# A gated delta rule scan in a two-layer encoder: its chunk attention matrices as 128x128 tiles

## The chip, the cores and the metric

The kernel runs as one program on one core of a Trainium2 chip. The metric is device microseconds (us) from start to end of one execution; the number of a kernel is the median of its runs. The chip's engines work side by side and each takes its own instructions in the order of the program: PE multiplies matrices (PEld is its loading of weights, which can run beside a product), DVE, ACT and POOL are the three engines for elementwise work, and SP issues most transfers. An engine that waits for another holds up everything behind it in its own order.

## The reference

Layer 0 is chunked softmax attention, layer 1 a gated DeltaNet; each is followed by a dense squared-ReLU MLP, with norms and residuals. The change is in layer 1. With 1024 frames in 16 chunks of 64, and 8 heads of width 128, its last step scans over the chunks:

```python
qk = jnp.einsum('bhnid,bhnjd->bhnij', q, k) * decay      # 64 x 64 for each head and chunk
...
def step(state, inp):
    u_c, w_c, qk_c, qd_c, kd_c, gl_c = inp
    v_new = u_c - jnp.einsum('bhck,bhkv->bhcv', w_c, state)
    o_c = jnp.einsum('bhck,bhkv->bhcv', qd_c, state) + jnp.einsum('bhij,bhjv->bhiv', qk_c, v_new)
    state = state * gl_c[..., None, None] + jnp.einsum('bhck,bhcv->bhkv', kd_c, v_new)
    return state, o_c
```

## The kernel before

Everything is float32. The dense products of layer 1 (the q, k, v and z panels, then two panels of the output matrix; tiles `acc`) take their operands as pairs of a high part and a remainder (`xhi`, `xlo`, `whi`, `wlo`): three products 128x512 in place of one. Between these dense products the code weaves small tasks, written as generators: `dn_prep_keys`, `dn_prep_queries` and `dn_prep_values` make a head's matrices, `dn_inverses` and `dn_solves` the triangular inverse (the solves are long runs of DVE work), `dn_scans` the scan, `dn_outs` the head's output. A planner (`turn`, `Clock`) decides after each dense product which task may go one step further, by its own estimate of each engine's time and by priorities; the order that it finds is fixed in the program. Two scans run interleaved, one over the even heads and one over the odd.

A chunk pair `p` has 128 frames: chunk `e = 0` lies on partitions 0 to 63 and `e = 1` on 64 to 127. One step of the scan (`dn_scans`) for a head and a chunk is:

- PE, "WQ product": `ps` (128x128, name `s1`, shown as `s<-st,WQ`) from the state `st`. One half of its rows is w times the state, the other half is q times the state. It opens an accumulation that is not yet closed.
- DVE, `vn<-vb,s`: the new values, from the w half of `ps`. `vn` has 128 rows, of which the other chunk's 64 are zero for good.
- PE, "kd product" (`s<-vn,kd`): into `s2`, for the next state.
- PE, "qk product" (`s<-vn,qk`): added to the other half of `ps`. Its weights are `qk[:, p]`, 128 partitions and 64 columns, the one chunk's block over the other's. The product therefore gives 64 rows, and `tile_position=(0, 64 - 64 * e)` says which half of the array's columns, and of `ps`'s rows, they take.
- DVE, `st<-st,gl,s`: the next state. ACT, `o<-s`: the finished half of `ps` to the output tile.

A float32 product 128x128 runs in two passes, so the profile counts two loads and two products for each. There are 8 heads and 16 chunks, so 128 qk products, 120 kd and 120 WQ products (the first chunk has no state, the last makes none). `dn_prep_queries` fills `qk` for a head: DVE multiplies the diagonal blocks of q times k by the decay, four operations for a head. `dn_gates` makes the tiles that live through the layer, and POOL fills them with zeros.

Of the kernel before, what the change touches and what calls it, by code (L numbers as in the profile page):

```python
# [7 lines left out]
F32 = mybir.dt.float32  # L8
# [3 lines left out]
ALU = mybir.AluOpType  # L12
# [4 lines left out]
P = 128  # L17
# [21 lines left out]
def wide(col, p, n):  # L39

    return col.rearrange("p (q o) -> p q o", o=1).broadcast_to([p, col.shape[-1], n])
# [164 lines left out]
class Trunk:  # L206
# [1499 lines left out]
    def dn_gates(self):  # L1706
        nc, a, rhs = self.nc, self.a, self.drhs
        d1, db = self.d1, self.db
# [18 lines left out]
        for v in self.vn:  # L1727
            for e in range(2):
                nc.gpsimd.memset(v[e][64 - 64 * e : 128 - 64 * e], 0.0)
        yield  # L1730
        abd = self.abd

# [3 lines left out]
        def t64(name):  # L1736
            used.append(name)
            return room[(len(used) - 1) // 8][:NQ, (len(used) - 1) % 8]
# [13 lines left out]
        x, y, z, z2, pz, be = t64("gx"), t64("gy"), t64("gz"), t64("gz2"), t64("gp"), t64("be")  # L1752
# [53 lines left out]
        ps = tp[:, :256].rearrange("p (n h q) -> p n h q", n=4, h=8)  # L1806
# [369 lines left out]
    def dn_prep_queries(self):  # L2176
        nc, db = self.nc, self.db
        for h in range(8):
            yield from self.until("q", h)
            qT = self.heads.pop(("q", h))  # L2180
            dc = self.dq.tile([P, HB], F32, name=self.nm("dc"), tag="dc").rearrange("p (q t) -> p q t", t=64)
            nc.sync.dma_start(dc, self.decay[h])
            if h == 0:
                yield from self.until("u", 6)
            row = self.whole("row")
            self.bcast(row, self.grow[2, h])

            v = self.d1.tile([P, 8], F32, name=self.nm("lv"), tag="lvq", bufs=2)
            yield from self.l2_sums(qT, 128.0 ** -0.5, v)
            yield from self.rsqrt_few(v, 8, "q")  # L2190
            self.heads["rq", h] = self.got
            yield from self.until("rk", h // 4)
            nc.gpsimd.tensor_tensor(dc, dc, wide(self.rk[:, h], P, 64), ALU.mult)
            yield
            yield from self.until("kn", h)
            kn = self.heads["kn", h]
            if h >= 2:
                yield from self.until("scan", h - 2)
            qk = db.tile([P, 8, 64], F32, name=self.nm("qk"), tag="qk")
            for q in range(2):  # L2200
                s = slice(4 * q, 4 * q + 4)
                tp = yield from self.take("tp")
                ps = tp.rearrange("p (q t) -> p q t", t=P)
                for t in range(4):
                    c = slice((4 * q + t) * P, (4 * q + t + 1) * P)
                    nc.tensor.matmul(ps[:, t], kn[:, c], qT[:, c], start=True, stop=True)
                yield
                for e in range(2):
                    r = slice(64 * e, 64 * e + 64)
                    nc.vector.tensor_tensor(qk[r, s], ps[r, :, r], dc[r, s], ALU.mult)  # L2210
                self.give("tp", tp)
                yield
            WQ = db.tile([P, 8, 4, 64], F32, name=self.nm("WQ"), tag="WQ")
            nc.gpsimd.tensor_tensor(
                WQ[:, :, 1:3], qT.rearrange("p (q e t) -> p q e t", e=2, t=64),
                row.rearrange("p (q e t) -> p q e t", e=2, t=64), ALU.mult)
            self.heads["qq", h] = WQ, qk
            self.mark("queries", h)
            self.mark("q", "used", h)
            yield  # L2220
# [44 lines left out]
    def dn_scans(self, odd):  # L2265

        nc, db = self.nc, self.db
        for h in range(odd, 8, 2):
            yield from self.until("values", h)
            u, WQ, qk, kd = self.heads.pop(h)  # L2270
            if h:
                yield from self.until(*(("solve", 1) if h == 1 else ("out", h - 2)))
            o = self.heads["o", h] = db.tile([P, 8, P], F32, name=self.nm("o"), tag="o")
            st = None
            for c in range(16):
                p, e = c // 2, c % 2
                r, x = slice(64 * e, 64 * e + 64), slice(64 - 64 * e, 128 - 64 * e)
                wq = WQ[:, p].rearrange("p f t -> p (f t)")[:, P * e : P * e + P]
                ps = yield from self.take("s1")
                vn = self.vn[odd][e]  # L2280
                if st is None:
                    nc.vector.tensor_copy(vn[r], u[r, p])
                else:
                    nc.tensor.matmul(ps, wq, st, start=True, stop=False, skip_group_check=True)
                    yield
                    nc.vector.tensor_tensor(vn[r], u[r, p], ps[r], ALU.subtract)
                yield
                if c < 15:
                    s2 = yield from self.take("s2")
                    nc.tensor.matmul(s2, kd[:, p], vn, start=True, stop=True)  # L2290
                ready = self.clock.end
                nc.tensor.matmul(ps[x], qk[:, p], vn, start=st is None, stop=True,
                                 tile_position=(0, 64 - 64 * e), skip_group_check=True)
                self.clock.end = ready
                yield
                if c < 15:
                    nst = db.tile([P, P], F32, name=self.nm("st"), tag=f"st{odd}")
                    if st is None:
                        nc.vector.tensor_copy(nst, s2)
                    else:  # L2300
                        nc.vector.scalar_tensor_tensor(nst, st, self.gl[:, h, c : c + 1], s2, ALU.mult, ALU.add)
                    self.give("s2", s2)
                    st = nst
                ready = self.clock.end
                nc.scalar.activation(o[r, p], ps[x], AF.Copy)
                self.give("s1", ps)
                self.clock.end = ready
                if c == 7:
                    self.done["half", h] = self.clock.now + 2.0
                yield  # L2310
            self.mark("scan", h)
            yield
# [180 lines left out]
```

## Time and profile before

| | us |
| --- | --- |
| median of 3 runs (2691.9 to 2694.18) | 2693.39 |
| the profiled execution | 2695.22 |
| its span, first to last instruction | 2693.4 |
| PE busy in the span | 2559.9 (95%) |
| PEld, DVE, ACT, POOL busy | 2068.5, 1884.9, 1224.6, 1302.7 |
| mean granted clock of PE | 0.982 of full speed |

The profiled execution lies 1.8 us above the median, and its span 1.8 us below its own time. Busy PE is modelled: products overlap, so a product's length in the profile says less than the distance from its start to the start of the next. The scan's steps lie between 1467 and 1913 us of the span; what follows is the output product and the second MLP.

### The profile page before, as it was taken

How to read it: one execution, taken by the hardware profiler on the slowest of the kernel's cores; microseconds unless marked ns; L12 is line 12 of the kernel's file. 1: busy time of each engine (PE TensorE's matmuls, PEld its weight loads, DVE VectorE, ACT ScalarE, POOL GpSimd, SP SyncE). 2: the span in 40 equal slices, each digit the busy share in tenths (PEclk: the TensorE clock that was granted, in tenths of full speed). 3: DMA queues.
4: the chain of work that ended last, by engine and by line, in shares of the span. 5: the costliest groups of instructions: out<-in, count | busy, mean ns of one | idle time of the engine just before them, and what ended most of it. 6: DMA issues, size and time to landing. Idle time of an engine off the chain costs nothing.

```text
span 2693.4 us, 36113 instructions
## 1 busy us (share of the span) xinstructions
PE 2559.9 (95%) x12638; PEld 2068.5 (77%) x12638; DVE 1884.9 (70%) x3287; ACT 1224.6 (45%) x2269; POOL 1302.7 (48%) x1096
## 2 busy tenths in 40 slices
PE   8999999989999999998888999999999999999997
PEld 6888888868888777776767778787677888777775
DVE  6666566575545999987398856665575544799997
ACT  6665667343434534444653333333334444444443
POOL 2443446143223788885554323222132223588886
PEclk9999999989999999999989999999999999999998
DMA  4222235223333432322642212112323332433322
GB/s 156 65 75 66 66 90 170 97 97 125 114 106 102 156 110 94 106 90 84 171 117 75 69 55 75 56 61 102 102 91 136 103 117 98 157 106 101 97 99 78
DMA packets 141814, 271.78 MB, mean 101 GB/s; under 512 B 49264, under 2 KB 55856, under 8 KB 141632
## 3 DMA queue, kind: packets, MB, share of 16 engines
q1 hardware_dynamic: 120752, 227.51, 27.0%
q10 hardware_dynamic: 20880, 41.97, 4.1%
q8 instruction: 99, 1.62, 0.3%
q14 instruction: 83, 0.68, 0.1%
HBM read 193.24 MB, written 67.80 MB: 97 GB/s over the span
## 4 chain that ended last, share of the span: by engine, by line
PE 75%; DVE 15%; issue 5%; ACT 2%; POOL 1%; DMA 1%; SPq 0%; DVEq 0%; ACTq 0%; POOLq 0%
PE y L1000 22%; PE acc L161 18%; PE z L1000 10%; PE acc L1000 6%; PE s L161 3%; PE tp L161 3%; PE po L161 2%; PE pt L161 2%; PE sp L161 2%; DVE x L1365 2%; DVE a L1006 2%; PE acc L272 2%; PE acc L273 2%; PE acc L271 2%; DVE ft L161 1%
## 5 line engine op out<-in xcount | busy, mean ns | idle before, releaser
L161 PE MATMUL acc<-xhi,whi 128*128 128x512 f32 (+1 forms) x904 | 375.1, 415 | 7.0 <-DVE xp L161 7.0
L161 PE MATMUL acc<-xlo,whi 128*128 128x512 f32 (+1 forms) x904 | 374.9, 415 | 0.7 <-DVE xlo L387 0.7
L161 PE MATMUL acc<-xhi,wlo 128*128 128x512 f32 x896 | 370.2, 413 | 2.0 <-POOL wlo L161 2.0
L1015 POOL TENSOR_TENSOR s<-wraw 128x256 f32<-128x256 f32 (+1 forms) x93 | 101.2, 1088 | 557.6 <-DMA wraw<-in_w_up_dram 398.9
L161 POOL TENSOR_TENSOR wlo<-wraw,whi 128x512 fp32r<-128x512 f32 x126 | 167.2, 1327 | 266.8 <-ACT whi L161 199.9
L1009 ACT ACTIVATE xhi<-r 128x512 fp32r<-128x512 f32 x224 | 135.8, 628 | 264.4 <-POOL r L1012 212.6
L1006 DVE TENSOR_TENSOR wlo<-wraw,whi 128x512 fp32r<-128x512 f32 (+1 forms) x184 | 201.7, 1096 | 51.6 <-ACT whi L1009 48.2
L1000 PE MATMUL y<-xhi,whi 128*128 128x512 f32 x504 | 202.8, 402 | 12.4 <-DVE ssum L1083 8.7
L1000 PE MATMUL y<-xhi,wlo 128*128 128x512 f32 x504 | 202.1, 401 | 13.0 <-DVE wlo L1006 13.0
L1012 POOL TENSOR_TENSOR r<-r,r 128x512 f32<-128x512 f32 x124 | 204.0, 1647 | 12.9 <-DVE xlo L1006 12.6
L1000 PE MATMUL y<-xhi,a 128*128 128x512 f32 x488 | 179.7, 409 | 25.6 <-DVE x L1365 25.1
L161 PEld LDWEIGHTS acc<-xhi,whi 128*128 128x128 f32 (+1 forms) x904 | 172.6, 191 | 38.6 <-issue 6.5
L1000 PE MATMUL y<-xlo,whi 128*128 128x512 f32 x504 | 201.6, 400 | 0.0
L161 PEld LDWEIGHTS acc<-xhi,wlo 128*128 128x128 f32 x896 | 172.3, 192 | 32.4 <-issue 5.1
L161 PEld LDWEIGHTS acc<-xlo,whi 128*128 128x128 f32 (+1 forms) x904 | 172.9, 191 | 30.2 <-issue 5.0
L1365 DVE TENSOR_TENSOR x<-y,x 128x512 f32<-128x512 f32 x240 | 163.8, 682 | 9.4 <-PE y L1000 7.8
L1009 ACT ACTIVATE whi<-wraw 128x512 fp32r<-128x512 f32 (+2 forms) x191 | 143.6, 766 | 34.8 <-ACT g L1086 11.8
L1083 DVE TENSOR_TENSOR ssum<-acc,nt 128x512 f32<-128x512 f32 x32 | 22.1, 692 | 190.4 <-PE acc L1000 190.4
L161 POOL TENSOR_SCALAR pr<-pr,rs 128x640 f32<-128x640 f32 (+4 forms) x128 | 88.3, 693 | 129.6 <-DVE rs L161 98.3
L1000 PEld LDWEIGHTS y<-xhi,a 128*128 128x128 f32 x488 | 91.5, 188 | 72.0 <-DVE x L1365 51.2
L161 POOL TENSOR_TENSOR cy<-cy,cz 128x512 f32<-128x512 f32 x48 | 69.0, 1437 | 159.6 <-DVE cz L161 133.0
L161 ACT ACTIVATE o<-s 64x128 f32<-64x128 f32 x128 | 34.7, 271 | 212.7 <-PE s L161 137.2
(348 smaller groups left out, 7186.0 us busy)
## 6 DMA issues: line engine op xcount, KB each, us to landing
wraw<-in_w_up_dram SPq DMA_DIRECT2D x64, 512.0 KB, 3.4
wraw<-in_w_down_dram SPq DMA_DIRECT2D x64, 512.0 KB, 3.9
r<-gd SPq DMA_DIRECT2D x112, 256.0 KB, 2.7
gd<-ssum ACTq DMA_DIRECT2D x64, 256.0 KB, 2.0
gd<-g ACTq DMA_DIRECT2D x64, 256.0 KB, 2.3
wraw<-in_w_in_dram SPq DMA_DIRECT2D x32, 512.0 KB, 3.5
wraw<-in_w_qkv_dram SPq DMA_DIRECT2D x30, 512.0 KB, 3.3
x<-xd SPq DMA_DIRECT2D x24, 512.0 KB, 4.8
```

The costliest lines, as they stand in the source:

```text
L161: return call(*args, **more)
L271: nc.tensor.matmul(ps, hi[:, k], xh, start=(k == 0), stop=False)
L272: nc.tensor.matmul(ps, hi[:, k], xl, start=False, stop=False)
L273: nc.tensor.matmul(ps, lo[:, k], xh, start=False, stop=(k == KT - 1))
L1000: nc.tensor.matmul(ps, w[:, k], x, start=bool(first and f), stop=bool(last and e), skip_group_check=True)
L1006: self.nc.vector.tensor_tensor(lo, src, hi.bitcast(F32), ALU.subtract)
L1009: self.nc.scalar.activation(hi, src, AF.Copy)
L1012: self.nc.gpsimd.tensor_tensor(out, x, y, ALU.subtract)
L1015: self.nc.gpsimd.tensor_tensor(out, x, y, ALU.add)
L1083: nc.vector.tensor_tensor(g, c, t, ALU.add)
L1365: nc.vector.tensor_tensor(x, ps, x, ALU.add)
```

## The change

The chunk attention matrices become 128x128. Two tiles `qk0` and `qk1` (P x 8 x 128) are made once in `dn_gates`, used by even and odd heads in turn, and replace the two-buffer tile `qk` (P x 8 x 64). Half of each is filled with zeros by POOL, two operations a tile. `dn_prep_queries` writes a chunk's 64x64 block beside the zeros: rows 0 to 63 in columns 64 to 127, rows 64 to 127 in columns 0 to 63. The qk product then has weights 128x128 and is added to the whole of `ps`: in the rows that it had before it adds what it added before, and in the other half, which DVE has read by then, it adds zeros.

```diff
+        self.qks = [d1.tile([P, 8, P], F32, name=f"qk{n}") for n in range(2)]
+        for qk in self.qks:
+            for e in range(2):
+                nc.gpsimd.memset(qk[64 * e : 64 * e + 64, :, 64 * e : 64 * e + 64], 0.0)
...
-            qk = db.tile([P, 8, 64], F32, name=self.nm("qk"), tag="qk")
+            qk = self.qks[h % 2]
...
-                    nc.vector.tensor_tensor(qk[r, s], ps[r, :, r], dc[r, s], ALU.mult)
+                    nc.vector.tensor_tensor(qk[r, s, 64 - 64 * e : P - 64 * e], ps[r, :, r], dc[r, s], ALU.mult)
...
-                nc.tensor.matmul(ps[x], qk[:, p], vn, start=st is None, stop=True,
-                                 tile_position=(0, 64 - 64 * e), skip_group_check=True)
+                nc.tensor.matmul(ps, qk[:, p], vn, start=st is None, stop=True, skip_group_check=True)
```

The order on PE in the middle of the scan, before (a row is an instruction, its output, its inputs and the output's partitions x columns; the numbers tell buffers apart):

```order
L161 MATMUL s_3362_15312<-vn_12203,kd_14835 128x128
L161 MATMUL s_3359_15299<-vn_12203,qk_14841 64x128
L161 MATMUL acc_15220<-xhi_11784,whi_14969 128x512
L161 MATMUL s_3364_15319<-st_15307,WQ_14261 128x128
L161 MATMUL acc_15220<-xlo_11785,whi_14969 128x512
L161 MATMUL acc_15220<-xhi_11784,wlo_14970 128x512
L161 MATMUL acc_15328<-xhi_11758,whi_14969 128x512
L161 MATMUL s_3367_15330<-st_15316,WQ_14956 128x128
L161 MATMUL s_3368_15332<-vn_12204,kd_14052 128x128
L161 MATMUL s_3364_15319<-vn_12204,qk_14058 64x128
```

and the same place now:

```order
L161 MATMUL s_3359_15315<-vn_12203,kd_14839 128x128
L161 MATMUL s_3356_15302<-vn_12203,qk_12210 128x128
L161 MATMUL acc_15223<-xhi_11784,whi_14972 128x512
L161 MATMUL s_3361_15322<-st_15310,WQ_14265 128x128
L161 MATMUL acc_15223<-xlo_11785,whi_14972 128x512
L161 MATMUL acc_15223<-xhi_11784,wlo_14973 128x512
L161 MATMUL acc_15331<-xhi_11758,whi_14972 128x512
L161 MATMUL s_3364_15333<-st_15319,WQ_14959 128x128
L161 MATMUL s_3365_15335<-vn_12204,kd_14057 128x128
L161 MATMUL s_3361_15322<-vn_12204,qk_12211 128x128
```

Nothing moved: each qk product stands where it stood and has 128 rows where it had 64. The same holds for every instruction of PE, DVE and ACT. The one difference in the order is on POOL, at the start of layer 1, where `dn_gates` fills its tiles (`vn` the values, `fz` the solve's matrix, `wlo` a remainder of weights). Before:

```order
L161 MEMSET vn_12204 64x128
L161 MEMSET vn_12205 64x128
L161 MEMSET fz_12275 128x1024
L161 MEMSET fz_12275 128x32
L161 TENSOR_TENSOR wlo_12280<-wraw_12126,whi_12279 128x512
```

and now:

```order
L161 MEMSET vn_12204 64x128
L161 MEMSET vn_12205 64x128
L161 MEMSET qk_12210 64x8x64 x2
L161 MEMSET qk_12211 64x8x64 x2
L161 MEMSET fz_12281 128x1024
L161 MEMSET fz_12281 128x32
L161 TENSOR_TENSOR wlo_12286<-wraw_12126,whi_12285 128x512
```

Four fills were put in, ahead of the solve's fills and of a remainder of weights.

## Rows read from the trace of the kernel before

**Rows 1.** Stretches: length, busy us of PE, PEld, DVE, ACT, POOL; clock; DMA.

```profile
1460.00:1500.00 40.00, 39.17 (x309) 32.36 (x305) 34.55 (x91) 14.67 (x30) 13.49 (x12) 1.00 0.20 57
1500.00:1540.00 40.00, 37.93 (x229) 27.99 (x228) 39.10 (x61) 11.36 (x22) 12.46 (x9) 1.00 0.11 34
1540.00:1890.00 350.00, 344.41 (x2129) 276.26 (x2128) 209.92 (x543) 122.90 (x271) 103.58 (x76) 1.00 0.22 72
1890.00:1913.00 23.00, 19.92 (x92) 13.72 (x91) 14.40 (x39) 8.19 (x20) 6.37 (x5) 0.93 0.41 126
```

**Rows 2.** PE timeline: start us, length us, instruction, passes; the place shown above.

```profile
1601.10 0.38 PE L161 MATMUL s<-vn,kd 128*128 128x128 f32 x2
1601.41 0.43 PE L161 MATMUL s<-vn,qk 128*64 128x128 f32 x2
1601.78 0.50 PE L161 MATMUL acc<-xhi,whi 128*128 128x512 f32 x1
1602.11 0.38 PE L161 MATMUL s<-st,WQ 128*128 128x128 f32 x2
1602.25 0.48 PE L161 MATMUL acc<-xlo,whi 128*128 128x512 f32 x1
1602.56 0.39 PE L161 MATMUL acc<-xhi,wlo 128*128 128x512 f32 x1
...
1603.03 0.38 PE L161 MATMUL s<-st,WQ 128*128 128x128 f32 x2
1603.24 0.39 PE L161 MATMUL s<-vn,kd 128*128 128x128 f32 x2
```

**Rows 3.** PE timeline, a qk product that another small product follows.

```profile
1869.93 0.43 PE L161 MATMUL s<-vn,qk 128*64 128x128 f32 x2
1870.29 0.49 PE L161 MATMUL s<-vn,kd 128*128 128x128 f32 x2
```

**Rows 4.** PEld timeline beside group 2: weight loads, idle time ahead in brackets.

```profile
1600.87 0.42 PEld L161 LDWEIGHTS s<-vn,kd 128*128 128x128 f32 x2
...
1601.41 0.19 PEld L161 LDWEIGHTS s<-vn,qk 128*64 128x64 f32 x2
1601.77 0.19 PEld L161 LDWEIGHTS acc<-xhi,whi 128*128 128x128 f32 x1 [0.17 <-issue]
```

**Rows 5.** Weight loads by tile: ns minimum/median/maximum, first and last start.

```profile
L161 PEld LDWEIGHTS s<-vn,qk x256: 132/136/232, 1467.8 to 1912.4; 128*64 128x64 f32 x128
L161 PEld LDWEIGHTS s<-vn,kd x240: 186/188/335, 1467.3 to 1909.2; 128*128 128x128 f32 x120
```

**Rows 6.** DVE timeline beside group 2: a state's update.

```profile
1601.52 0.35 DVE L161 SCALAR_TENSOR_TENSOR st<-st,gl,s 128x128 f32<-128x128 f32 x1 [1.04 <-PE s L161]
```

**Rows 7.** Waits of PE, 1540 to 1890 us: total us, times, longest.

```profile
PE s L161 <- DVE vn L161: 3.1, 3, 1.5
PE s L161 <- DVE rt L161: 2.5, 1, 2.5
```

**Rows 8.** POOL timeline where dn_gates fills its tiles.

```profile
1244.14 1.84 POOL L161 MEMSET Zh<- 128x1024 f32 x2
1246.04 0.92 POOL L161 MEMSET vn<- 64x128 f32 x4
...
1248.53 1.28 POOL L161 TENSOR_TENSOR wlo<-wraw,whi 128x512 fp32r<-128x512 f32 x1 [0.46 <-ACT whi L161]
```

**Rows 9.** PE timeline: the first product that reads this wlo.

```profile
1263.00 0.39 PE L161 MATMUL acc<-xhi,wlo 128*128 128x512 f32 x1
```

**Rows 10.** DVE groups by line: us busy, mean ns, idle ahead.

```profile
L161 DVE TENSOR_TENSOR qk<-tp,dc 64x256 f32<-64x256 f32 x32 | 13.4, 420 | 5.0 <-PE tp L161 4.7
L161 DVE TENSOR_TENSOR vb<-tp,gcols 128x512 f32<-128x512 f32 x16 | 11.0, 687 | 5.8 <-PE tp L161 5.6
```

**Rows 11.** PE timeline, the first qk product, which opens its own accumulation.

```profile
1467.81 0.43 PE L161 MATMUL s<-vn,qk 128*64 128x128 f32 x2
1468.17 0.50 PE L161 MATMUL acc<-xlo,whi 128*128 128x512 f32 x1
```

## The prediction

> **What bounds the kernel now.** The change touches the scan alone, so I read the stretch in which the scan runs, 1460 to 1913 us, first by busy time [rows 1]. From 1540 to 1890 us PE is busy 344.41 of 350 us, DVE 209.92, ACT 122.90 and POOL 103.58, at the full clock. PE is the bound there, and time taken from PE is time taken from the kernel, as long as the others keep up. From 1500 to 1540 us it is different: DVE is busy 39.10 of 40 us, because the second triangular solve runs, and PE with 37.93 is level with it. From 1460 to 1500 us PE is ahead (39.17 against 34.55). From 1890 us on PE is idle for 3.1 of 23 us: the dense work runs out and the last head's steps wait for each other.
>
> Second, the waits of PE from 1540 to 1890 us [rows 7]: four waits, 5.6 us in all, each for DVE. So 98% of the stretch is PE's own.
>
> Third, PE's timeline around a qk product, read by starts, since busy lengths overlap [rows 2]. A kd product starts at 1601.10, the qk product at 1601.41, the dense product behind it at 1601.78, and what follows that at 1602.11. These distances are 0.31, 0.37 and 0.33 us, 1.01 in all. Now the same with a full-width product of the same type: from the WQ product at 1603.03 to kd at 1603.24 are 0.21, from WQ at 1602.11 to the dense product at 1602.25 are 0.14, and from there to the next at 1602.56 are 0.31. So a half-width product starts later, runs longer and delays what comes behind it.
>
> Fourth, the loads of weights at the same place [rows 4]. The full-width load of kd begins at 1600.87, before its product at 1601.10: it runs beside the dense product ahead. The half-width load begins with its product, at 1601.41, when kd is done, and the dense load behind it sits idle 0.17 us for nothing the profile shows. On both sides of the half-width product nothing is loaded ahead. I read this as the array being emptied whenever the shape of its tiles changes.
>
> **The change part by part.**
>
> *The qk product takes the whole array.* It then has the shape, type and passes of kd and WQ, so I price it by their rows. Where a dense product follows, the three distances go from 1.01 to 0.21 + 0.14 + 0.31 = 0.66 us. I take 0.34 us saved, since other places of the timeline read 0.34 as often as 0.35. In the program's order this is so for 96 of the 128. In the other 32 a small product follows: a kd in 15, as here [rows 3], elsewhere a WQ, a product or transpose of the preparation, or in 2 another qk. From qk at 1869.93 to kd at 1870.29 are 0.36 us; with the 0.31 ahead of it 0.67, against twice 0.21 for full-width products; 0.25 saved. The sum for PE alone is 96 x 0.34 + 32 x 0.25 = 40.6 us, or 0.317 for a product.
>
> Where these products lie, counted by their passes in the four stretches of [rows 1]: 7, 6, 107 and 8. The 40.6 us so divide into 2.2, 1.9, 33.9 and 2.5.
>
> *What of it the end sees.* From 1500 to 1540 us DVE has 0.9 us to give; I take 0.5 of the 1.9. From 1460 to 1500 us I take 1.5 of the 2.2. From 1890 us on the chain WQ, `vn`, kd, `st` sets the pace and qk is beside it; I take 1.0 of the 2.5. In the long stretch a wait can grow where a qk product stood between DVE's work and its reader on PE, because the reader now comes sooner. In [rows 6] a state is ready at 1601.87 and its WQ product starts at 1602.11, 0.24 us later, with one qk product between. Under the change that product comes at 1601.10 + 0.66 = 1601.76, before the state is there: a new wait of about 0.1 us. Of the 101 WQ products of that stretch, counted in the timeline, five have 0.24 us to spare with a qk product between, two have 0.30, and the others with one between 0.66 or more; a kd product with under 0.4 us to spare has none between. That is 1 us of new waits. At the four waits of [rows 7] DVE is behind with its own work, and what PE gains in the run-up is lost there: some 0.4 us each, 1.5 together. So 33.9 - 2.5 = 31.4 us, and in all 1.5 + 0.5 + 31.4 + 1.0 = 34.4.
>
> *Loads of full width.* Each load grows from 136 to 188 ns [rows 5], 256 of them by 52 ns, 13.3 us of PEld. I cost this at nothing, as PEld is busy 276 of 350 us [rows 1] and kd's full-width loads run beside the dense products [rows 4]. Without that cover it is the whole 13.3.
>
> The Trainium skill speaks against the change here. Its page "TensorE: Matmul & The Clock Gate", section "LDWEIGHTS (loading the stationary operand)", says that a load's time goes by its columns alone; as an estimate from that page 64 more columns cost 53 ns at 1.2 GHz, and the rows agree with it. By that rule alone the sum would be a loss of 13 us.
>
> *Zeros.* POOL fills four times 64 partitions x 512 elements. The nearest rows are 0.23 us for `vn` (128 elements) and 0.92 for `Zh` (1024) [rows 8]; four of them cost 0.9 to 3.7 us, about 2. Behind them in POOL's queue stand the solve's fills and a remainder of weights, written by 1249.81; PE reads that at 1263.00 [rows 9]. With 13 us to spare it costs nothing; without them 2 us.
>
> *The copy into `qk`.* The same 256 elements now go to blocks 128 apart; the input was strided already. It takes 420 ns [rows 10]. Between no change and the 687 ns of an operation with twice the elements, 32 copies cost DVE 0 to 8.5 us. I take 0, the elements being the same, and the upper end would fall mostly in stretches where DVE is idle 40%.
>
> *The zeros added to the other half of `ps`* need a wait for DVE's reading, but the kd product just ahead on PE waits for the same `vn` already. The order on PE, DVE and ACT is unchanged, so no queue is passed.
>
> **The rivals.**
>
> *DVE takes over.* PE gets faster by a tenth where products are dense, and DVE with its in-order work stops PE more often. For: from 1500 to 1540 us it does, and all waits of [rows 7] are for DVE. Against: it is 60% busy in the long stretch. If half of the 33.9 is lost, the gain is 17 + 3 = 20 us: 2673.
>
> *The distances don't come from the tile's shape* but from adding to an accumulation that another product opened. For: qk does that each time, kd never. Then the change gains nothing: 2693. Against: the very first qk product opens its own accumulation, and the dense product behind it still starts 0.36 us later [rows 11].
>
> *The load becomes the path.* A full-width load that stands between two products of one `vn` does not fit beside a product of two short passes, and PE waits for it. At 52 ns a load, with nothing won, 2693 + 13 = 2707. It decides only if the load can't start before the product ahead has ended. Against: from WQ to kd are 0.21 us [rows 2], with two loads of 188 ns in them, so it starts before.
>
> The Trainium skill has one more on this side. Its page "TensorEngine Tiling (Array Packing)", section "Overview", gives up to twice the speed where the stationary free dimension is at most 64, as it is before. By that the half-width form should be the better one; in this case two halves never run at once, because a full-width product lies between nearly all of them.
>
> **How the numbers follow.** The forecast is 2693.4 - 34.4 = 2659 us; for a profiled execution like the one before 2695.2 - 34.4 = 2661. I give it 0.80, for gains from 27 to 42. DVE taking over, gains from 6 to 27, has 0.12; no effect 0.04; the load 0.04. The range goes from all of 40.6 and about 1 more, 2652, to the time of DVE taking half, 2673. A measurement of this kernel can tell about 0.2% from no change, 5.4 us. Faster 0.92, same 0.04, slower 0.04.
>
> **What would show it.** In the profile after, the distance from the start of a qk product to the dense product behind it should read 0.14 us, and kd to qk 0.21; qk's loads should read 188 ns and start before their product; PEld's idle behind qk should be gone. The scan should end some 34 us sooner, and everything behind it keep its length. Waits of PE for `vn` and `st` should total under 10 us in the long stretch. It is wrong if the distances stay, or if PE's waits for DVE grow by more than 10 us.

## The result and the profile after

The kernel after took 2659.49 us in the median of four runs (2656.81 to 2660.27), the kernel before 2692.74 on the same chip (2691.9 to 2694.18): a ratio of 0.987, 95% interval 0.9855 to 0.9884. The forecast was 2659. In the profiled execution the span fell from 2693.4 to 2657.9 us.

First PE's timeline of the kernel after, at the place of [rows 2]: start us, length us, instruction, passes.

```profile
1594.58 0.38 PE L161 MATMUL s<-vn,kd 128*128 128x128 f32 x2
1594.80 0.39 PE L161 MATMUL s<-vn,qk 128*128 128x128 f32 x2
1594.94 0.48 PE L161 MATMUL acc<-xhi,whi 128*128 128x512 f32 x1
1595.26 0.38 PE L161 MATMUL s<-st,WQ 128*128 128x128 f32 x2
```

kd to qk is now 0.22 us (0.31 in [rows 2]), qk to the dense product 0.14 (0.37), and from there to the next product 0.32 (0.33). The sum is 0.68 against 1.01. Where another small product follows, as in [rows 3], it looks like this:

```profile
1838.18 0.39 PE L161 MATMUL s<-vn,qk 128*128 128x128 f32 x2
1838.40 0.39 PE L161 MATMUL s<-vn,kd 128*128 128x128 f32 x2
```

0.22 us, against 0.36. Next the weight loads at the first of these places, which answer to [rows 4]:

```profile
1594.36 0.42 PEld L161 LDWEIGHTS s<-vn,kd 128*128 128x128 f32 x2
1594.69 0.30 PEld L161 LDWEIGHTS s<-vn,qk 128*128 128x128 f32 x2
1594.92 0.19 PEld L161 LDWEIGHTS acc<-xhi,whi 128*128 128x128 f32 x1
```

The load of qk begins 0.11 us ahead of its product, beside the second pass of kd, and the idle 0.17 us in front of the dense load is gone. Third, all instructions on the tile `qk`: nanoseconds minimum/median/maximum, first and last start, form.

```profile
L161 PEld LDWEIGHTS s<-vn,qk x256: 187/192/333, 1468.1 to 1876.2; 128*128 128x128 f32 x128
L161 PE MATMUL s<-vn,qk x256: 270/275/421, 1468.2 to 1876.3; 128*128 128x128 f32 x128
L161 DVE TENSOR_TENSOR qk<-tp,dc x32: 402/422/429, 1437.0 to 1819.7; 64x256 f32<-64x256 f32 x32
```

A load takes 192 ns where it took 136 [rows 5]; DVE's copy into blocks 128 apart takes 422 ns, which [rows 10] gives as a mean of 420. The load of the last qk product starts 36.2 us sooner than in [rows 5] (1876.2 against 1912.4).

PE's instructions have the same order and number in both kernels, so the two traces can be laid side by side instruction by instruction; the distances between starts then show where time left. The stretches of [rows 1] correspond to these four of the kernel after (same columns: length, busy us of PE, PEld, DVE, ACT, POOL, clock, DMA):

```profile
1460.40:1498.00 37.60, 36.78 (x308) 32.01 (x305) 35.37 (x90) 14.72 (x30) 13.58 (x12) 1.00 0.22 61
1498.00:1539.40 41.40, 36.13 (x229) 27.77 (x228) 40.47 (x61) 10.93 (x22) 12.41 (x9) 1.00 0.10 31
1539.40:1855.20 315.80, 308.91 (x2129) 271.48 (x2128) 210.45 (x544) 123.26 (x270) 103.53 (x76) 1.00 0.25 81
1855.20:1876.50 21.30, 17.62 (x93) 13.95 (x92) 14.44 (x39) 8.30 (x19) 7.13 (x6) 0.92 0.47 137
```

The third holds the same 2129 products as the third of [rows 1], in 315.8 us instead of 350. DVE and POOL do the same work in it, and PE is still busy 98% of it. By the finer laying side by side, which compares the two profiled executions (the medians of all runs lie 33.25 us apart):

| stretch of before | forecast gain | measured gain | of it at qk and the two products behind | lost to longer waits |
|---|---|---|---|---|
| 1460 to 1540 | 1.5 + 0.5 | 2.36 - 1.36 = 1.0 | 4.4 | 3.6 |
| 1540 to 1890 | 31.4 | 34.15 | 34.4 | 1.5 |
| 1890 to 1913 | 1.0 | 1.7 | 2.6 | 0.8 |
| all else | 0 | -1.3 | 0 | |
| sum | 34.4 | 35.6 | | |

In the second row 34.4 less 1.5 is 32.9. The other 1.2 us were not gained at the qk products, and mostly not by the change: in the execution of before the granted clock was 0.57 from 1847.5 to 1851.5 us, behind PE's wait of 2.5 us for `rt` [rows 7], and eight distances between products there are 0.2 us longer than after, most of them 0.43 us at the lower of the clock's two levels (1.2 GHz) instead of 0.23 at the upper (2.4 GHz). In the execution after, the clock is 1.00 through the same place, behind a wait of 2.8 us.

The waits of PE in the long stretch (total us, times, longest), against [rows 7]:

```profile
PE s L161 <- DVE vn L161: 4.0, 3, 2.0
PE s L161 <- DVE rt L161: 2.8, 1, 2.8
```

They are the same four waits, 0.9 and 0.3 us longer. And those of the solve's stretch, first before, 1500 to 1540 us, then after, 1498 to 1539.4 us (a wait of 1.0 us for `xp` is in both):

```profile
PE s L161 <- DVE vn L161: 0.5, 1, 0.5
PE s L161 <- DVE st L161: 0.3, 1, 0.3
...
PE s L161 <- DVE st L161: 2.9, 5, 1.2
PE s L161 <- DVE vn L161: 1.2, 1, 1.2
```

Here DVE is busy 40.47 of 41.40 us, and what PE saves it waits.

### The profile page after: what moved, and what is told of

Read it like the earlier page. It is cut to its first block, busy times and chain, and to the rows that moved or that the text cites. A ratio compares the mean times of both kernels' runs of the same rounds, so it can differ in the third digit from the quotient of the medians.

```text
span 2657.9 us, 36117 instructions
## 1 busy us (share of the span) xinstructions
PE 2514.9 (95%) x12638; PEld 2062.5 (78%) x12638; DVE 1890.5 (71%) x3287; ACT 1225.5 (46%) x2269; POOL 1305.2 (49%) x1100
## 4 chain that ended last, share of the span: by engine, by line
PE 73%; DVE 15%; issue 5%; DMA 2%; ACT 2%; POOL 2%; SPq 0%; DVEq 0%; ACTq 0%; POOLq 0%
PE y L1000 22%; PE acc L161 17%; PE z L1000 10%; PE acc L1000 6%; PE tp L161 3%; PE s L161 3%; PE po L161 2%; PE pt L161 2%; PE sp L161 2%; DVE x L1365 2%; PE acc L272 2%; PE acc L271 2%; PE acc L273 2%; DVE a L1006 2%; DVE ft L161 1%
## 5 line engine op out<-in xcount | busy, mean ns | idle before, releaser
L1000 PE MATMUL y<-xhi,a 128*128 128x512 f32 x488 | 180.2, 410 | 23.6 <-DVE x L1365 23.0
L1004 POOL TENSOR_TENSOR xlo<-r,xhi 128x512 fp32r<-128x512 f32 x84 | 109.1, 1299 | 41.6 <-ACT xhi L1009 40.9
```

The lines of the kernel that those rows point to most:

```text
L1000: nc.tensor.matmul(ps, w[:, k], x, start=bool(first and f), stop=bool(last and e), skip_group_check=True)
L1004: self.nc.gpsimd.tensor_tensor(lo, src, hi.bitcast(F32), ALU.subtract)
```

## The experiments

The theory on trial is that of the prediction: a half-width product between full-width ones stops the loading ahead and the overlap of products, on its way in and on its way out, and this is what the 0.34 us are. The rivals on trial: the layout of `qk`, its zeros or the copy; adding to an accumulation that another product opened; a price of the product itself that each one pays; and the width alone, at any number of columns.

**The tile with zeros, the product of half width.** From the kernel after:

```diff
-                nc.tensor.matmul(ps, qk[:, p], vn, start=st is None, stop=True, skip_group_check=True)
+                nc.tensor.matmul(ps[x], qk[:, p, x], vn, start=st is None, stop=True,
+                                 tile_position=(0, 64 - 64 * e), skip_group_check=True)
```

> The changed kernel with the qk product put back to its old form: 64 columns, cut out of the new 128x128 tiles, with the tile position. The zeros, the new tiles and DVE's strided copy stay. Theory (the cost lies in the product's tile shape): the whole gain goes, 2693 us, kd to qk 0.31 us again. Rival (the gain came from the new tiles, their place in memory or the waits that they change): 2659.

2692.7 us, ratio 0.9989 (0.9978 to 0.9999). Its PE timeline:

```profile
1602.99 0.38 PE L161 MATMUL s<-vn,kd 128*128 128x128 f32 x2
1603.30 0.43 PE L161 MATMUL s<-vn,qk 128*64 128x128 f32 x2
1603.66 0.50 PE L161 MATMUL acc<-xhi,whi 128*128 128x512 f32 x1
```

The distances of before are back, 0.31 and 0.36, and with them the time. The zeros, the copy to blocks 128 apart and the two fixed tiles are worth at most 0.2%; the gain is all in the product.

**Full width for the odd chunks only.**

```diff
-                nc.tensor.matmul(ps, qk[:, p], vn, start=st is None, stop=True, skip_group_check=True)
+                if e:
+                    nc.tensor.matmul(ps, qk[:, p], vn, start=st is None, stop=True, skip_group_check=True)
+                else:
+                    nc.tensor.matmul(ps[x], qk[:, p, x], vn, start=st is None, stop=True,
+                                     tile_position=(0, 64 - 64 * e), skip_group_check=True)
```

> The changed kernel with the old form for the chunks e = 0 and the new one for e = 1, 64 products each. Theory (each half-width product pays for itself): half of the gain goes, 2659.5 + 17 = 2676 us, between 2673 and 2680. Rival (the gain needs the scan to be free of other shapes, or comes once): 2693 or 2659.

2676.04 us, ratio 0.9921 (0.9902 to 0.9941). Half of the products give half of the gain: 16.7 us of 33.2. So the gain is a sum over products, and each of the two positions of the half-width tile costs alike.

**An accumulation of its own for each qk product**, in the kernel before:

```diff
-                nc.tensor.matmul(ps[x], qk[:, p], vn, start=st is None, stop=True,
+                nc.tensor.matmul(ps[x], qk[:, p], vn, start=True, stop=True,
```

> The kernel before with the qk product opening its own accumulation in place of adding to that of the WQ product; the part of the output that comes from the state is lost. Theory (tile shape): 2693 us, kd to qk 0.31, qk to dense 0.36. Rival (adding to an open accumulation costs the time): 2659, kd to qk 0.21.

2692.3 us, ratio 0.9994 (0.9984 to 1.0004). In its timeline kd stands at 1601.26, qk at 1601.58 and the dense product at 1601.94, 0.32 and 0.36 apart. Adding to an open accumulation has no part in the delay.

**The half-width product twice**, in the kernel before:

```diff
-                nc.tensor.matmul(ps[x], qk[:, p], vn, start=st is None, stop=True,
+                nc.tensor.matmul(ps[x], qk[:, p], vn, start=st is None, stop=False,
                                  tile_position=(0, 64 - 64 * e), skip_group_check=True)
+                nc.real.tensor.matmul(ps[x], qk[:, p], vn, start=False, stop=True,
+                                 tile_position=(0, 64 - 64 * e), skip_group_check=True)
```

> The kernel before with each half-width qk product issued twice in a row, so that its part of the output counts double; the planner does not see the second, and the order is otherwise that of before. Theory (the array is emptied where the shape changes, at the first's start and the last's end): the second costs only its two passes, between 0.22 and 0.32 us, so 128 of them 28 to 41 us, less what waits hide: 2720 to 2733. Rival (each half-width product is slow in itself): 0.54 us each, 2755 to 2762.

2714.17 us, ratio 1.0065 (1.0046 to 1.0084): 21 us more, less than either side expected. PE's timeline at one of the places (L2294 is the line that issues the second product):

```profile
1610.53 0.39 PE L161 MATMUL s<-vn,kd 128*128 128x128 f32 x2
1610.85 0.43 PE L161 MATMUL s<-vn,qk 128*64 128x128 f32 x2
1611.12 0.38 PE L2294 MATMUL s<-vn,qk 128*64 128x128 f32 x2
1611.43 0.50 PE L161 MATMUL acc<-xhi,wlo 128*128 128x512 f32 x1
```

And the weight loads there:

```profile
1611.01 0.25 PEld L2294 LDWEIGHTS s<-vn,qk 128*64 128x64 f32 x2
1611.43 0.19 PEld L161 LDWEIGHTS acc<-xhi,wlo 128*128 128x128 f32 x1 [0.17 <-issue]
```

From kd to the dense product are 0.90 us, against 0.68 in [rows 2]: the second product adds 0.22. The 0.32 on the way in and the idle 0.17 on the way out stand there once for the pair, and the second product's load starts 0.11 us ahead of it. 128 times 0.22 are 28 us; the 107 products of the long stretch alone make 23.5, so the theory's number missed by counting the products elsewhere, where PE isn't the bound, and by a price at its upper end that no place shows. That the cost is paid once for the visit stands, and the rival that each product pays its own price (2755 us or more) falls.

The second product here uses the same half of the array as the first. What two products in different halves do, the trace of before shows in the two places where the qk products of both scans stand side by side, with no edit:

```profile
1723.79 0.39 PE L161 MATMUL s<-vn,kd 128*128 128x128 f32 x2
1724.11 0.44 PE L161 MATMUL s<-vn,qk 128*64 128x128 f32 x4
1724.48 0.50 PE L161 MATMUL acc<-xlo,whi 128*128 128x512 f32 x1
```

The four passes are two products, one in each half, and take 0.44 us, where the two passes of one take 0.43 [rows 2]. From kd to the dense product are 0.69 us, 0.68 at the other place (1831.60 to 1832.28), against 0.68 with a single half-width product. The two halves run at the same time there. In the kernel after the same two places take 0.59 us (1705.13 to 1705.72, and 1803.92 to 1804.51), so even then two full-width products, one behind the other, are the shorter form.

**The full-width product twice**, in the kernel after:

```diff
-                nc.tensor.matmul(ps, qk[:, p], vn, start=st is None, stop=True, skip_group_check=True)
+                nc.tensor.matmul(ps, qk[:, p], vn, start=st is None, stop=False, skip_group_check=True)
+                nc.real.tensor.matmul(ps, qk[:, p], vn, start=False, stop=True, skip_group_check=True)
```

> The changed kernel with each full-width qk product issued twice (its part of the output counts double); order otherwise unchanged. Theory: a full-width product costs 0.21 to 0.22 us wherever it stands, so 128 more cost 27 to 28 us, less a few in stretches where DVE is the bound: 2683 to 2687, still under the kernel before with its single half-width product. Rival (the full-width product was cheap because it used up time in which PE waited anyway): under 2675.

2683.06 us, ratio 0.9964 (0.995 to 0.9978): two full-width products are cheaper than one of half width. One more full-width product in each place costs 23.6 us, and one more half-width product behind a first, in the same half, cost 21: in such a row a half-width product is no dearer, and hardly cheaper, than a full-width one.

**48 columns**, in the kernel before; in all but the first chunk of a head 16 of 64 rows are left out:

```diff
-                nc.tensor.matmul(ps[x], qk[:, p], vn, start=st is None, stop=True,
+                m = 48 if st is not None else 64
+                y = slice(x.start, x.start + m)
+                nc.tensor.matmul(ps[y], qk[:, p, :m], vn, start=st is None, stop=True,
```

> The kernel before with 48 columns in place of 64 in the qk products of all chunks but a head's first, at the same tile position; 16 of 64 output rows of each chunk are left out. In the trace of before, dense products of 48 columns at the start of layer 1 stand 0.23 us apart and show no delay at either end. Theory as I hold it (any product on part of the columns empties the array): 2693 us, kd to qk 0.31. Rival (only a width that fills a tile of the array, or a place off column 0, does it): 2665 to 2676, kd to qk 0.21 for at least half of the products.

2690.2 us, ratio 0.9992 (0.9983 to 1.0001). In its timeline kd stands at 1598.91, qk at 1599.22, the dense product at 1599.57. Fewer columns in the load (122 ns a load, 136 before) buy 0.01 us, 0.35 instead of 0.36 from qk to the dense product.

**96 columns for the odd chunks**, in the kernel after:

```diff
-                nc.tensor.matmul(ps, qk[:, p], vn, start=st is None, stop=True, skip_group_check=True)
+                m = 96 if e else P
+                nc.tensor.matmul(ps[:m], qk[:, p, :m], vn, start=st is None, stop=True, skip_group_check=True)
```

> The changed kernel with 96 of the 128 columns in the qk products of the chunks e = 1, which need only 64; no tile position. Theory (the tile shape counts, not the width): as the changed kernel, 2659 us, kd to qk 0.21 for all. Rival (fewer than 128 columns cost the time): up to half of the gain goes, 2668 to 2677.

2659.65 us, ratio 0.9874 (0.9859 to 0.9888). PE's timeline:

```profile
1595.26 0.38 PE L161 MATMUL s<-vn,kd 128*128 128x128 f32 x2
1595.48 0.38 PE L161 MATMUL s<-vn,qk 128*96 128x128 f32 x2
1595.62 0.48 PE L161 MATMUL acc<-xhi,whi 128*128 128x512 f32 x1
```

And the load of qk there:

```profile
1595.37 0.27 PEld L161 LDWEIGHTS s<-vn,qk 128*96 128x96 f32 x2
```

0.22 and 0.14 us, with the load 0.11 us ahead: a product of 96 columns goes in with the full-width ones, and a width under 128 alone does not cost. Each product's instruction in the built program carries a tile size, made from its shape whether a tile position is written or not: 128x128 for 96 columns as for 128, and 128x64 for 64 columns and for 48. So in the experiments up to here the delay goes with the tile size.

**One pass in place of two.** One thing in the trace of before spoke against the theory. Dense products of 48 columns, which carry the tile size 128x64 too, follow dense products of 128 there, and nothing is delayed:

```profile
1238.53 0.40 PE L1000 MATMUL y<-xhi,wlo 128*128 128x512 f32 x1
1238.77 0.39 PE L161 MATMUL acc<-xhi,whi 128*48 128x512 f32 x1
1238.99 0.39 PE L161 MATMUL acc<-xlo,whi 128*48 128x512 f32 x1
```

They are one-pass products of the rounded type, the scan's are two-pass products of full precision. So two kernels wrote `vn` and `qk` in the rounded type and took qk in one pass: from the kernel before the odd chunks' half-width product alone, from the kernel after every product at full width. The first, in part (its other lines give `vn` and `qk` the rounded type):

```diff
-                nc.tensor.matmul(ps[x], qk[:, p], vn, start=st is None, stop=True,
-                                 tile_position=(0, 64 - 64 * e), skip_group_check=True)
+                if e:
+                    nc.tensor.matmul(ps[x], qk[:, p], vn, start=st is None, stop=True, skip_group_check=True)
+                else:
+                    nc.tensor.matmul(ps[x], qk[:, p].bitcast(F32), vn.bitcast(F32), start=st is None, stop=True,
+                                     tile_position=(0, 64 - 64 * e), skip_group_check=True)
```

> From the kernel before: `qk` and `vn` are written in the single-pass type, and the qk product of the odd chunks (position 0) is one pass of half width, 64 columns; that of the even chunks stays a half-width product of two passes at position 64, on the same values. The values are rounded by this, and the planner orders the dense work a little otherwise, so the distances are to be read here, not the time. The question is why the dense products of 48 columns at 1238 us stand at the usual distance of 0.23 us with their loads ahead, where the scan's half-width products don't. Theory that the array is emptied for two-pass products only: kd to the odd chunks' qk starts at 0.21 us as at full width, its load starts ahead of it, and the sum from kd to the dense product behind qk is within 0.03 us of that in the kernel with the full-width single-pass product. Theory that any half-width product between full-width ones empties it, whatever its type, and the 48-column products escape for another reason: kd to qk at 0.31 us for both kinds of chunk, and from kd to the dense product at least 0.15 us more than at full width with a single pass.

> The counterpart from the kernel after: `qk` and `vn` in the single-pass type, and every qk product one pass over the full 128 columns. The values are rounded and the order of the dense work differs a little, so distances are read, not the time. All theories: kd to qk 0.21 us (two passes of kd), and qk to the dense product behind it 0.05 to 0.14 us, since one pass is left of the two that gave 0.14.

PE's timeline of the half-width kernel, first a place with two odd chunks' products, then one with two even ones:

```profile
1601.75 0.38 PE L161 MATMUL s<-vn,kd 128*128 128x128 f32 x2
1601.88 0.30 PE L161 MATMUL s<-vn,qk 128*64 128x128 f32 x1
1602.02 0.44 PE L161 MATMUL s<-vn,kd 128*128 128x128 f32 x2
1602.22 0.30 PE L161 MATMUL s<-vn,qk 128*64 128x128 f32 x1
1602.36 0.44 PE L161 MATMUL acc<-xhi,wlo 128*128 128x512 f32 x1
...
1604.72 0.38 PE L161 MATMUL s<-vn,kd 128*128 128x128 f32 x2
1605.03 0.43 PE L161 MATMUL s<-vn,qk 128*64 128x128 f32 x2
...
1606.17 0.50 PE L161 MATMUL acc<-xlo,whi 128*128 128x512 f32 x1
```

And of the full-width kernel, two odd or even chunks alike:

```profile
1600.79 0.38 PE L161 MATMUL s<-vn,kd 128*128 128x128 f32 x2
1600.93 0.31 PE L161 MATMUL s<-vn,qk 128*128 128x128 f32 x1
1601.07 0.44 PE L161 MATMUL s<-vn,kd 128*128 128x128 f32 x2
1601.27 0.30 PE L161 MATMUL s<-vn,qk 128*128 128x128 f32 x1
1601.41 0.45 PE L161 MATMUL acc<-xhi,wlo 128*128 128x512 f32 x1
```

In one pass the half-width pair takes 0.61 us from the first kd to the dense product, the full-width pair 0.62; in two passes the half-width pair takes 1.45. From 1540 to 1860 us the median from kd to the dense product is 0.279 us (half, one pass, 29 places), 0.282 (full, one pass, 82 places), 0.676 (half, two passes, 41 places of the same run as the first). The one-pass products of the odd chunks carry the same tile size and place in the array, 128x64 at column 0, as the two-pass ones of the kernel before. So it takes the tile of half width and the two-pass product together to cost the time here.

Type and passes change together in these two kernels, so which of the two decides stays open. The trace of before has two more narrow products that bear on it, transposes of full precision in one pass with the tile size 128x32. One stands among dense products at 1453.60 us: its load starts 0.21 us ahead of it, at 1453.39, and the dense product behind it follows at 1453.63, so nothing is delayed. That speaks for the passes, but a transpose may be a case of its own, and transposes on half of the array's rows (64x128, one pass) do show something: behind the last, at 1276.07 us, the load of the dense product starts with that product, at 1276.22, and not ahead of it.

The distance from kd to the one-pass product, 0.14 us instead of the 0.21 that both theories had, was not foreseen either. It is the same in both kernels, so the width does not make it; a one-pass product stands 0.14 us behind a two-pass one in [rows 2] too (WQ at 1602.11, dense at 1602.25).

The full-width kernel took 2653.78 us in a single execution, less than the kernel after, so it was timed too:

> The kernel with the full-width qk product in one pass again, now timed against the kernel before: as the qk products of the kernel after take 0.36 us from kd's second pass to the dense product behind them and here one pass of 0.11 us less, 128 products and 107 of them in the stretch that PE bounds give about 12 us at most over the kernel after, of which the one profiled execution showed about 6; so 2647 to 2656 us, ratio 0.983 to 0.987. The values of `vn` and of the attention matrices are rounded to the single-pass type, so this is a trade of precision for time and not the same computation. A rival, that the other order of the dense work takes the gain back: 2659 us as for the kernel after.

2656.29 us, just past the range, ratio 0.9866 (0.985 to 0.9882). That interval and the kernel after's lie almost on each other, so it can't be told from the kernel after. The places themselves are 0.08 us shorter each, where 0.11 were expected, some 8 us in the long stretch. That stretch shows part of where they went (columns as in [rows 1]):

```profile
1540.00:1860.00 320.00, 309.96 (x2043) 267.82 (x2041) 209.26 (x557) 126.09 (x276) 110.92 (x79) 0.98 0.26 86
```

The granted clock is 0.98 in the long stretch, a mean of its two levels of 2.4 and 1.2 GHz, where the kernel after has 1.00. As an estimate from these rows, 2% of 320 us is 6 us. The order of its dense work differs as well, so the split between the two is open. It rounds `vn` and the attention matrices for nothing that can be measured; the kernel after remains the better of the two.

## Why the prediction was right, point by point

*What bounds.* PE was taken as the bound of the long stretch, and the stretch shrank by what PE saved: 34.4 us at the qk products, of which longer waits took back 1.5. DVE, at 210.45 of 315.8 us, did not take over.

*The price of a product.* Forecast 0.34 us with a dense product behind and 0.25 with a small one. Measured by medians of kd's start to the next product's start: 0.676 to 0.362 with a dense one, to which the dense product behind adds 0.02 (0.335 to 0.315), so 0.33; 0.676 to 0.443 with a kd or WQ behind, 0.23. Both a little under, since kd to qk is 0.22 and not 0.21. The two places with another qk behind were priced at 0.25 a product as well and gave 0.10 for the pair (0.69 to 0.59): the prediction says that two halves never run at once here, and there they do.

*What the end sees.* In the long stretch 2.5 us were set aside for new waits and 1.5 came: 1.2 of the 1.5 at the four places of [rows 7], and 0.3 of the 1.0 elsewhere. That makes 32.9 instead of 31.4; the 34.15 of the two executions has 1.2 us more, for the most part by the clock, which no term of the prediction stands for. In the two stretches with the solve, 2.0 were taken and 1.0 came. The 1.5 us of the first arrived (2.36) and the second gave 1.36 back, since DVE is the bound there and what PE brings in early is waited for: that term was mis-sized, by not following the first stretch's gain into the second. The tail gave 1.7 instead of 1.0. The errors cancel to 1.2 of 34.4 us in these two executions, and in the medians to 1.15 the other way (33.25 us of gain). That the sum came out this near is in part luck.

*What was costed at nothing.* The loads: 56 ns more for each, 14 us for 256, hidden, as they run beside PE and beside each other; PEld is busy 271.48 of 315.80 us, where it was 276.26 of 350. The rule of the Trainium skill ("TensorE: Matmul & The Clock Gate", "LDWEIGHTS (loading the stationary operand)") agrees with the trace in size, 136 to 192 ns, with a granted clock of 1.00 in that stretch; the loss of 13 us that it alone would give did not come. The copy: 422 ns, as before. The zeros: four fills of 518 ns, 2.19 us in POOL's queue, with the remainder of weights behind them:

```profile
1246.57 2.19 POOL L161 MEMSET qk<- 64x512 f32 x4
...
1249.92 1.29 POOL L161 TENSOR_TENSOR wlo<-wraw,whi 128x512 fp32r<-128x512 f32 x1
```

It starts 1.39 us later than in [rows 8] and ends at 1251.2, with the first reader some 12 us off [rows 9].

*The mechanism.* The prediction had the array "emptied whenever the shape of its tiles changes". The pair of half-width products pays the way in and out once, so it is the change that costs and not the product: shown. The Trainium skill states it likewise ("TensorEngine Tiling (Array Packing)", "Key Properties": changing the tiling mode, and not merely the tile, drains the engine), and the trace agrees with it at 48 and 64 columns in two passes. It does not agree in one pass, where 48 or 64 columns, with the same tile size 128x64, go through with no delay (at 64 columns 0.279 us against 0.282). So the prediction's "whenever" is too wide, and why one pass escapes stays open. The 96 columns are no counterexample, since their tile is 128x128. That what happens inside is an emptying is inferred from starts and loads; no row shows the array.

## What to carry to other kernels

A two-pass product that uses half of the array's columns is not half a product. Look at the distances between starts around it and at the idle of the weight loads behind it; where these are longer than around full-width products of the same kind, zeros beside the block are cheaper than the narrow tile, as long as the wider loads run beside other products and the engine is the bound there. A product in one pass had nothing to gain from it here. If the narrow form must stay, put such products in a row, since a row pays once, and let neighbours use different halves: two such ran at the same time. Before counting the gain, mark the stretches where another engine is level with this one: there the saving of the stretch ahead is given back.

## What the runs showed that was not expected

- A second half-width product behind a first in the same half adds 0.22 us, no more than a full-width one; the price is 0.33 for the visit, not for the product.
- Two half-width products in different halves run at the same time: 0.69 us from kd to the dense product, against 0.68 with one. Two full-width ones take 0.59.
- In one pass, 64 columns between full-width products cost nothing (0.279 us against 0.282); in two passes 0.676 against 0.362.
- A two-pass product of 96 columns behaves as one of 128 (0.22 and 0.14 us), whose tile size it has, one of 48 as one of 64 (0.31 and 0.35).
- Two full-width products where one of half width was made the kernel 0.36% faster.
